# A two-layer trunk on one core: feed-forward activations and HGRN's heads turned by VectorE and DRAM in place of TensorE, and a new rule in the schedule

## The chip, the cores and the metric

The kernel runs on one core of one Trainium2 chip. The metric is device time in microseconds of one execution; the median of several executions is given. A profile is one execution recorded by the hardware profiler; its engines are PE (TensorE matmul), PEld (TensorE weight load), DVE (VectorE), ACT (ScalarE), POOL (GpSimd) and SP (SyncE, which issues DMAs).

## The reference

Input is x of 256 tokens by 2048 features, float32, batch 1. Two layers, each a token mixer and a SwiGLU feed-forward, each with RMSNorm before and a residual add behind, then one final RMSNorm:

```python
h = x
for layer in range(2):
    if layer == 0:
        h = h + gdn_mixer(rmsnorm(h, gdn_norm), ...)      # gated DeltaNet, 32 value heads of 128
    else:
        h = h + hgrn2_mixer(rmsnorm(h, hgrn_norm), ...)   # HGRN2, 16 heads of 128
    h = h + (silu(n @ w_gate) * (n @ w_up)) @ w_down      # n = rmsnorm(h, ffn_norm[layer]); inner width 5632
return rmsnorm(h, final_norm)
```

Both mixers project h, compute a chunked recurrence per head, normalize each head's output (`rmsnorm(o, head_norm) * silu(gate)`) and multiply it by an output matrix of their own.

## The kernel before, in words

All weights (some 500 MB) stream once from DRAM through SBUF. They come in *halves* of 128x1024 float32, loaded by SP's queue into four buffers `raw`. ScalarE copies a half to float32r (`wh`), VectorE subtracts (`wl = raw - wh`), four buffers each; TensorE multiplies high by high, high by low and low by high. `stream` loops over all groups of halves in the order of the computation and records load and split of a half three halves (`AHEAD`) before its matmuls. One half is 12 matmuls of 512 columns (row groups) or 24 of 256 (column groups, in which the weights stand still and the tokens move).

An activation that is multiplied next must stand with its features on partitions, split into a high and a low part as well: `xt_h`, `xt_l` for the normalized input, `ht` (`hth`, `htl` in the profile) for the feed-forward's inner activations, `ot_h`, `ot_l` for the mixers' heads. The turn from tokens on partitions to features on partitions is a TensorE transpose against the identity in tile `head`, block by block of 128x128, into a PSUM tile `aux`, from which ScalarE and VectorE write the two parts.

- `ffn`: 22 gate-up groups `gate_up(gi)` of four halves give 256 inner features each, in two parts (`FF_PARTS`, 12 and 10 groups); after each part four groups `down(part, cg)` of 12 or 10 halves multiply them, 512 output columns each. `gate_up`'s `end` runs ScalarE's Silu (`sg`) and VectorE's product (`h1`, the tile printed as `h`), and for every second group eight transposes `aux<-head,h` and the split of both groups' `ht`.
- `hgrn`: four head groups of projections f, q, v, gate; `hgrn_o` multiplies scores by values into `o`, and `head_out` normalizes the heads into `zs`, transposes them (eight `aux<-head,zs`) and splits them with the head norm as scale. Two output projections of four column groups follow.
- `gdn`: eight head groups in the order `GDN_ORDER`; `gdn_o` calls the same `head_out`.
- The residual lives in DRAM (`x_home`): `load_x` and `add_x` load and store 128x2x512 tiles through Pool's queue.

The order of instructions isn't that of the source. A `Recorder` takes down all operations; `plan` then simulates the five engines with fixed costs and gives out each engine's order. An operation gets a due time `late`, from the main stream of matmuls back through its successors; an engine takes of its ready operations the one due first. A DMA on Pool's queue counts 0.75 to issue and 6.5 to land (`ISSUE`, `LANDING`), and 0.2 (`HOP`) for a handover between engines. The engines then run in order, each in the planned sequence: an instruction that waits holds what is behind it. Nearly all instructions are issued in one place, so nearly all lines of the profile are L489 and the tile names tell them apart.

Of the kernel before, what the change touches and what calls it, by code (L numbers as in the profile page):

```python
# [17 lines left out]
P = 128  # L18
# [9 lines left out]
MASKED = (8, 4, 2, 1)  # L28
AHEAD = 3
RAW_BUFS = 4  # L30
SPLIT_BUFS = 4
# [47 lines left out]
class Op:  # L79
    __slots__ = ("eng", "method", "args", "kw", "cost", "lag", "main", "pred", "succ", "n", "late", "call", "tiles", "heirs", "share")  # L80

    def __init__(self, eng, method, args, kw, cost=0.0, lag=0.0, main=False):
        self.eng, self.method, self.args, self.kw = eng, method, args, kw
        self.cost, self.lag, self.main = cost, lag, main
        self.pred, self.succ = {}, []
        self.call, self.tiles, self.heirs = None, [], []
        self.share = 1.0


# [58 lines left out]
class Recorder:  # L148
    ENGINES = ("tensor", "vector", "scalar", "gpsimd", "sync")

    def __init__(self, scratch):
        self.scratch, self.tiles, self.ops, self.pools = scratch, {}, [], []
        self.last_main, self.wanted = None, []
        for e in self.ENGINES:
            setattr(self, e, Engine(self, e))
# [44 lines left out]
    def add(self, eng, method, args, kw):  # L200
        op = Op(eng, method, args, kw)
        op.n = len(self.ops)
        for other in self.wanted:
            self.edge(other, op)
# [102 lines left out]
    def plan(self):  # L307
# [22 lines left out]
        order = []  # L330
        table, streaming = None, False
        starved = {}
# [45 lines left out]
        while len(order) < len(ops):  # L378
# [127 lines left out]
class Trunk:  # L506
# [79 lines left out]
    def stream(self, groups):  # L586
# [10 lines left out]
        def load(n):  # L597
            g, i = flat[n]
            raw = self.tile(self.wraw, [P, 1024], "raw", ordered=True)
            nc.sync.dma_start(raw, g.halves[i])  # L600
            if n == 0:
# [5 lines left out]
            nc.vector.tensor_tensor(out=low, in0=raw, in1=h.bitcast(F32), op=ALU.subtract)  # L607
            ready[n] = (h, low)

        loaded = 0  # L610
        for n, (g, i) in enumerate(flat):
            while loaded < min(n + AHEAD, len(flat)):
                load(loaded)
                loaded += 1
            if i == 0:
                if g.begin:
                    g.begin()
                g.ps = self.apart() if g.apart else self.main()
            g.mm(g.ps, i, *ready.pop(n))
            if i == len(g.halves) - 1:  # L620
                g.end(g.ps)

    def mm_rows(self, ps, i, wh, wl, n_chunks, operand, halves=range(2)):

        for k in range(2):
            xh, xl = operand(2 * i + k)
            cols = slice(k * 512, (k + 1) * 512)
            for tt in halves:
                tok = slice(tt * P, (tt + 1) * P)
                out = ps[tt] if isinstance(ps, tuple) else ps[:, tt, :]  # L630
                for m, (s, w) in enumerate(((xh, wh), (xh, wl), (xl, wh))):
                    self.nc.tensor.matmul(
                        out, s[:, tok], w[:, cols],
                        start=(i == 0 and k == 0 and m == 0),
                        stop=(i == 2 * n_chunks - 1 and k == 1 and m == 2),
                    )
# [14 lines left out]
    def mm_cols(self, ps, i, wh, wl, n_k, n_f, n_chunks):  # L651

        for k in range(n_k):
            kt = i * n_k + k
            xh, xl = self.operand(kt)
            for f in range(n_f):
# [9 lines left out]
    def mm_gates(self, ps, i, wh, wl):  # L666
        for kt in range(16):
            xh, xl = self.operand(kt)
            at = slice(kt * 64, (kt + 1) * 64)
# [5 lines left out]
    def operand(self, kt):  # L675
        return self.xt_h[kt // 4][:, kt % 4, :], self.xt_l[kt // 4][:, kt % 4, :]

# [37 lines left out]
    def make_xt(self, cg, norm):  # L715
# [11 lines left out]
        for pair, ps in enumerate(two):  # L727
            for k in range(2):
# [4 lines left out]
                )  # L733

    def x_cols(self, x, cg):
        if x is self.a["x"]:
# [28 lines left out]
    def ffn(self, j, after):  # L765
        nc, a = self.nc, self.a
        hts, h1s = {}, {}

        def gate_up(gi):
            def end(ps):  # L770
                h1 = self.tile(self.pool, [P, 2, T], "h1", bufs=4)
                for tt in range(2):
# [13 lines left out]
                two = self.aux(), self.aux()  # L786
                nc.together(*two)
                for of, tr in enumerate(two):
                    for k in range(2):
                        for tt in range(2):  # L790
# [4 lines left out]
                for of, tr in enumerate(two):  # L795
                    ht, lt = (t[:, 2 * of : 2 * of + 2, :].rearrange("p a t -> p (a t)") for t in pair)
                    nc.scalar.activation(ht, tr, AF.Copy)
                    nc.vector.tensor_tensor(out=lt, in0=tr, in1=ht.bitcast(F32), op=ALU.subtract)

# [6 lines left out]
        def down(part, cg):  # L806
            first = sum(FF_PARTS[:part]) // 2
            n = FF_PARTS[part] // 2
            w = a[f"ffn_d{j}_{part}"]

            def operand(kt):
                h, l = hts[first + kt // 4]
                return h[:, kt % 4, :], l[:, kt % 4, :]

# [362 lines left out]

    def head_out(self, o, zs, scale, norm):

# [31 lines left out]
        for tt in range(2):  # L1211
            for h in range(4):
# [4 lines left out]
                )  # L1217
        oh, ol = (t([P, 4, T], f"ot_{x}", dt=F32R, bufs=3) for x in "hl")
        two = self.aux(), self.aux()
        nc.together(*two)  # L1220
        for b, tr in enumerate(two):
            for h in range(2):
                for tt in range(2):
                    nc.tensor.transpose(
                        tr[:, h * T + tt * P : h * T + (tt + 1) * P],
                        zs[:, tt, (2 * b + h) * P : (2 * b + h + 1) * P], self.ident,
                    )
        for b, tr in enumerate(two):
            s = slice(2 * b, 2 * b + 2)
            self.split_scaled(  # L1230
                oh[:, s, :].rearrange("p h t -> p (h t)"), ol[:, s, :].rearrange("p h t -> p (h t)"),
                tr, norm,
            )
# [88 lines left out]
    def out_proj(self, name, p, states, last, after):  # L1322
# [5 lines left out]
        def operand(kt):  # L1328
            h, l = two[kt // 4]["ot"]
            return h[:, kt % 4, :], l[:, kt % 4, :]  # L1330

# [214 lines left out]
    def hgrn_o(self, g, st):  # L1546
# [4 lines left out]
        for tok in range(2):  # L1551
            for h in range(4):
# [6 lines left out]
                )  # L1559
        st["ot"] = self.head_out(o, st["zs"], 0.5, self.hgrn_hn)  # L1560

# [192 lines left out]
```

## Time and profile before

| | |
|---|---|
| median of 3 executions | 2806.14 us (2805.82 to 2806.21) |
| the profiled execution | 2807.59 us, its span 2805.9 us |
| TensorE busy | 2786.4 us (99%) |
| VectorE, ScalarE, Pool busy | 1732.2, 1426.7, 251.3 us |
| granted clock of TensorE | 0.997 |
| DMA | 580.42 MB, mean 207 GB/s |

The span goes from the first to the last instruction; the execution's time has a little around it. Stages, read off the tile names: DeltaNet to about 820 us, feed-forward to about 1555, HGRN to about 2070, the second feed-forward to the end. A matmul's duration in the timeline covers its way through the array, so that neighbours overlap; the distance between starts is what one costs in a row. A group's "busy" is the union of its instructions' durations.

### The profile page before, as it was taken

To read this page: it belongs to the slowest core of one execution; us is meant where nothing else is said; L and a number is where in the kernel's file an instruction comes from. 1 tells how busy PE (TensorE), PEld (TensorE's weight loads), DVE (VectorE), ACT (ScalarE), POOL (GpSimd) and SP (SyncE) were. 2 spreads that over 40 slices of the span, in tenths; PEclk is the share of its full clock that TensorE was granted. 3 is DMA by queue.
4 is the path that set the end of the run, shared out by engine and by line. 5 is a ranking of instruction groups with operands and counts; after the bars stand their busy time and mean duration, and the time that the engine had idled before them with its cause. 6 is when DMAs were issued, how large, how long until landed. Compare 5 with 4: busy or idle time off the path is not lost.

```text
span 2805.9 us, 40816 instructions
## 1 busy us (share of the span) xinstructions
PE 2786.4 (99%) x15710; PEld 2374.5 (85%) x15710; DVE 1732.2 (62%) x2498; ACT 1426.7 (51%) x2016; POOL 251.3 (9%) x366
## 2 busy tenths in 40 slices
PE   9999999999999999999999999999999999999998
PEld 9988888887888888888888989989888888888887
DVE  6777888877755555445555677677555454454554
ACT  6646666564554444344444556556454444344443
POOL 1212222232110000000000100000100000000000
PEclk9999999999999999999999999999999999999999
DMA  7686678677776555665556645545775556665564
GB/s 254 199 274 210 211 226 261 215 220 241 239 221 211 192 189 188 225 222 190 188 189 218 215 163 170 173 160 165 246 258 191 191 188 207 222 208 189 189 199 158
DMA packets 162659, 580.42 MB, mean 207 GB/s; under 512 B 20138, under 2 KB 21306, under 8 KB 162336
## 3 DMA queue, kind: packets, MB, share of 16 engines
q1 hardware_dynamic: 138912, 503.15, 54.5%
q0 software_dynamic: 23264, 73.81, 8.4%
q8 instruction: 123, 2.02, 0.3%
q10 hardware_dynamic: 288, 0.85, 0.1%
q14 instruction: 72, 0.59, 0.1%
HBM read 550.42 MB, written 27.31 MB: 206 GB/s over the span
## 4 chain that ended last, share of the span: by engine, by line
PE 98%; DVE 1%; ACT 0%; issue 0%; DMA 0%; POOL 0%; SPq 0%; POOLq 0%; ACTq 0%
PE main L489 91%; PE aux L489 7%; ACT dec L489 0%; DMA first<-in_x 0%; DVE wl L489 0%; DVE utmp L489 0%; ACT wh L489 0%; DVE x L489 0%; DVE u L489 0%; DVE zs L489 0%; POOL ocol L489 0%; SPq L489 0%; DVE pre L489 0%; ACT xt_h L489 0%; DVE r L489 0%
## 5 line engine op out<-in xcount | busy, mean ns | idle before, releaser
L489 DVE TENSOR_TENSOR wl<-raw,wh 128x1024 fp32r<-128x1024 f32 x945 | 1158.2, 1226 | 982.8 <-ACT wh L489 980.6
L489 ACT ACTIVATE wh<-raw 128x1024 fp32r<-128x1024 f32 x945 | 1000.6, 1060 | 1260.8 <-PE main L489 1214.0
L489 PE MATMUL main<-wl,xt_h 128*128 128x512 f32 x2176 | 850.2, 391 | 2.7 <-DVE wl L489 2.7
L489 PE MATMUL main<-wh,xt_h 128*128 128x512 f32 x2176 | 852.0, 392 | 0.4 <-ACT wh L489 0.4
L489 PE MATMUL main<-wh,xt_l 128*128 128x512 f32 x2176 | 850.1, 391 | 0.0
L489 PEld LDWEIGHTS main<-wl,xt_h 128*128 128x128 f32 x2176 | 409.0, 188 | 86.5 <-DVE wl L489 3.5
L489 PEld LDWEIGHTS main<-wh,xt_h 128*128 128x128 f32 x2176 | 409.1, 188 | 83.9 <-ACT wh L489 0.8
L489 PEld LDWEIGHTS main<-wh,xt_l 128*128 128x128 f32 x2176 | 408.9, 188 | 83.8
L489 PE MATMUL main<-xt_h,wl 128*128 128x256 f32 (+1 forms) x1040 | 292.9, 282 | 0.9 <-DVE wl L489 0.9
L489 PE MATMUL main<-xt_l,wh 128*128 128x256 f32 (+1 forms) x1040 | 292.4, 281 | 0.3 <-DVE xt_l L489 0.3
L489 PE MATMUL main<-xt_h,wh 128*128 128x256 f32 (+1 forms) x1040 | 290.5, 279 | 0.0
L489 PE MATMUL main<-wh,hth 128*128 128x512 f32 x664 | 259.0, 390 | 0.0
L489 PE MATMUL main<-wh,htl 128*128 128x512 f32 x664 | 258.9, 390 | 0.0
L489 PE MATMUL main<-wl,hth 128*128 128x512 f32 x664 | 258.6, 390 | 0.0
L489 PEld LDWEIGHTS main<-xt_h,wh 128*128 128x128 f32 (+1 forms) x1040 | 196.0, 188 | 0.5 <-ACT wh L489 0.2
L489 PEld LDWEIGHTS main<-xt_h,wl 128*128 128x128 f32 (+1 forms) x1040 | 194.1, 187 | 1.3 <-DVE wl L489 1.1
L489 PEld LDWEIGHTS main<-xt_l,wh 128*128 128x128 f32 (+1 forms) x1040 | 194.0, 187 | 0.9 <-DVE xt_l L489 0.5
L489 PE MATMUL main<-wh,ot_l 128*128 128x512 f32 x384 | 151.9, 396 | 0.5 <-DVE ot_l L489 0.5
L489 PE MATMUL main<-wh,ot_h 128*128 128x512 f32 x384 | 151.5, 395 | 0.3 <-ACT ot_h L489 0.3
L489 PE MATMUL main<-wl,ot_h 128*128 128x512 f32 x384 | 150.8, 393 | 0.0
L489 PEld LDWEIGHTS main<-wh,hth 128*128 128x128 f32 x664 | 124.7, 188 | 25.7
L489 PEld LDWEIGHTS main<-wl,hth 128*128 128x128 f32 x664 | 124.7, 188 | 25.6
(209 smaller groups left out, 2181.7 us busy)
## 6 DMA issues: line engine op xcount, KB each, us to landing
raw<-in_ffn_gu SPq DMA_DIRECT2D x352, 512.0 KB, 3.6
raw<-in_ffn_d SPq DMA_DIRECT2D x176, 512.0 KB, 3.8
raw<-in_hgrn_in SPq DMA_DIRECT2D x128, 512.0 KB, 3.7
raw<-in_gdn_kq SPq DMA_DIRECT2D x64, 512.0 KB, 5.0
raw<-in_gdn_v SPq DMA_DIRECT2D x64, 512.0 KB, 4.5
raw<-in_gdn_z SPq DMA_DIRECT2D x64, 512.0 KB, 5.0
raw<-in_gdn_out SPq DMA_DIRECT2D x64, 512.0 KB, 4.7
x_home<-x POOLq DMA_DIRECT2D x36, 512.0 KB, 4.9
```

Source lines behind the costliest of these rows:

```text
L489: getattr(getattr(tc.nc, op.eng), op.method)(*args, **kw)
```

## The change

Three things change.

1. A new function `turn` replaces TensorE's transposes for the feed-forward (per gate-up group, no longer per pair) and for HGRN's heads. VectorE transposes all 32x32 blocks of a 128x512 (feed-forward) or 128x1024 (HGRN) tile into `blocks`; Pool's queue stores `blocks` to a DRAM tile `rows`, and four more DMAs of that queue, one for each band of 32 partitions, load it back over the source tile. ScalarE and VectorE then write the two parts from SBUF, through a view in runs of 32. For HGRN the values tile `v` serves as `blocks`, and the low part is written in four instructions. DeltaNet keeps its transposes, grouped by token half in place of head pair.
2. The turned tiles are laid out by token half ([128, 2, n, 128]), and the views that hand them to the matmuls follow that.
3. In `plan`, each split of a weight half carries the number of its half. ScalarE and VectorE take a ready split first if its half is at most one (`SOON`) past the half whose matmul was placed last. And a DMA on SP's queue of less than a fifth of a half counts 0.1 in place of 0.45.

```diff
@@ plan
-            op = heapq.heappop(ready[e])[2] if ready[e] else mains.pop()
+            soon = [x for x in ready[e] if x[2].half is not None and x[2].half <= half + SOON]
+            if soon and e in ("scalar", "vector"):
+                soon = min(soon, key=lambda x: x[2].half)
+                ready[e].remove(soon)
+                heapq.heapify(ready[e])
+                op = soon[2]
+            else:
+                op = heapq.heappop(ready[e])[2] if ready[e] else mains.pop()
...
+            if op.main:
+                half = op.half
...
-            clock[e] = at + max(0.45, LOAD_EVERY * op.share) if e == "sync" else done
+            clock[e] = at + max(0.1 if op.share < 0.2 else 0.45, LOAD_EVERY * op.share) if e == "sync" else done
@@ new
+    def turn(self, x, blocks):
+        nc = self.nc
+        width = x.shape[1] // 4
+        nc.vector.transpose(
+            blocks.rearrange("p (c a j) -> p a c j", c=4, j=32), x.rearrange("p (a c i) -> p a c i", c=4, i=32)
+        )
+        rows = self.tile(self.dram, [4, P, width], f"rows{width}", bufs=3)
+        nc.gpsimd.dma_start(rows.rearrange("c p a -> p c a"), blocks.rearrange("p (c a) -> p c a", c=4))
+        for c in range(4):
+            nc.gpsimd.dma_start(
+                x[32 * c : 32 * c + 32].rearrange("i (q a) -> i q a", q=4),
+                rows[c].rearrange("(q i) a -> i q a", q=4),
+            )
+        return x.rearrange("p (q a j) -> p a q j", q=4, j=32)
@@ ffn, gate_up
-                h1s[gi] = h1
-                if gi % 2 == 0:
-                    return
-                pair = hts[gi // 2] = tuple(
-                    self.tile(self.pool, [P, 4, T], f"ht{x}", F32R, bufs=max(FF_PARTS) // 2) for x in "hl"
-                )
...
-                            nc.tensor.transpose(
-                                tr[:, k * T + tt * P : k * T + (tt + 1) * P],
-                                h1s[gi - 1 + of][:, tt, k * P : (k + 1) * P], self.ident,
-                            )
...
+                blocks = self.tile(self.pool, [P, 512], "blocks", bufs=2)
+                turned = self.turn(h1.rearrange("p t c -> p (t c)"), blocks)
+                hts[gi] = ht, lt = tuple(
+                    self.tile(self.pool, [P, 2, 2, P], f"ht{x}", F32R, bufs=max(FF_PARTS)) for x in "hl"
+                )
+                as_turned = lambda x: x.rearrange("p t n (q j) -> p (t n) q j", q=4)
+                nc.scalar.activation(as_turned(ht), turned, AF.Copy)
+                nc.vector.tensor_tensor(
+                    out=as_turned(lt), in0=turned, in1=as_turned(ht.bitcast(F32)), op=ALU.subtract
+                )
@@ head_out, for HGRN
+        turned = self.turn(zs.rearrange("p t c -> p (t c)"), blocks)
+        as_turned = lambda x: x.rearrange("p t n (q j) -> p (t n) q j", q=4)
+        nc.scalar.activation(as_turned(oh), turned, AF.Copy, scale=norm)
+        for q in range(4):
+            nc.vector.scalar_tensor_tensor(
+                out=as_turned(ol)[:, :, q], in0=turned[:, :, q], scalar=norm,
+                in1=as_turned(oh.bitcast(F32))[:, :, q], op0=ALU.mult, op1=ALU.subtract,
+            )
```

More of the change, by code (lines that the diff above doesn't have):

```diff
@@ L29 @@
 AHEAD = 3
+SOON = 1
 RAW_BUFS = 4
@@ L79 @@
 class Op:
-    __slots__ = ("eng", "method", "args", "kw", "cost", "lag", "main", "pred", "succ", "n", "late", "call", "tiles", "heirs", "share")
+    __slots__ = ("eng", "method", "args", "kw", "cost", "lag", "main", "pred", "succ", "n", "late", "call", "tiles", "heirs", "share", "half")
     def __init__(self, eng, method, args, kw, cost=0.0, lag=0.0, main=False):
@@ L87, in __init__ @@
         self.share = 1.0
+        self.half = None
 class Virtual:
@@ L202, in add @@
         op.n = len(self.ops)
+        op.half = self.half
         for other in self.wanted:
@@ L330, in plan @@
         order = []
-        table, streaming = None, False
+        table, streaming, half = None, False, 0
         starved = {}
@@ L600, in load @@
             nc.sync.dma_start(raw, g.halves[i])
+            nc.half = n
             if n == 0:
@@ L607, in load @@
             nc.vector.tensor_tensor(out=low, in0=raw, in1=h.bitcast(F32), op=ALU.subtract)
+            nc.half = None
             ready[n] = (h, low)
@@ L618, in stream @@
                 g.ps = self.apart() if g.apart else self.main()
+            nc.half = n
             g.mm(g.ps, i, *ready.pop(n))
+            nc.half = None
             if i == len(g.halves) - 1:
@@ L632, in mm_rows @@
                     self.nc.tensor.matmul(
-                        out, s[:, tok], w[:, cols],
+                        out, s[:, tt, :], w[:, cols],
                         start=(i == 0 and k == 0 and m == 0),
@@ L654, in mm_cols @@
             kt = i * n_k + k
-            xh, xl = self.operand(kt)
+            xh, xl = (x.rearrange("p t j -> p (t j)") for x in self.operand(kt))
             for f in range(n_f):
@@ L667, in mm_gates @@
         for kt in range(16):
-            xh, xl = self.operand(kt)
+            xh, xl = (x.rearrange("p t j -> p (t j)") for x in self.operand(kt))
             at = slice(kt * 64, (kt + 1) * 64)
@@ L675, in operand @@
     def operand(self, kt):
-        return self.xt_h[kt // 4][:, kt % 4, :], self.xt_l[kt // 4][:, kt % 4, :]
+        return tuple(x[kt // 4][:, kt % 4, :].rearrange("p (t j) -> p t j", t=2) for x in (self.xt_h, self.xt_l))
     def sumsq(self, cg):
@@ L806, in down @@
         def down(part, cg):
-            first = sum(FF_PARTS[:part]) // 2
+            first = sum(FF_PARTS[:part])
             n = FF_PARTS[part] // 2
@@ L1217, in head_out @@
                 )
[L1218 to L1223, printed above, removed]
+        oh, ol = (t([P, 2, 4, P], f"ot_{x}", dt=F32R, bufs=3) for x in "hl")
+        if blocks is None:
+            two = self.aux(), self.aux()
+            nc.together(*two)
+            for tt, tr in enumerate(two):
+                for h in range(4):
                     nc.tensor.transpose(
-                        tr[:, h * T + tt * P : h * T + (tt + 1) * P],
-                        zs[:, tt, (2 * b + h) * P : (2 * b + h + 1) * P], self.ident,
-                    )
[L1228 to L1232, printed above, removed]
+                        tr[:, h * P : (h + 1) * P], zs[:, tt, h * P : (h + 1) * P], self.ident
+                    )
+            for tt, tr in enumerate(two):
+                s = lambda x: x[:, tt].rearrange("p n j -> p (n j)")
+                self.split_scaled(s(oh), s(ol), tr, norm)
+            return oh, ol
+        turned = self.turn(zs.rearrange("p t c -> p (t c)"), blocks)
[5 more added lines that the diff above has]
+                in1=as_turned(oh.bitcast(F32))[:, :, q], op0=ALU.mult, op1=ALU.subtract,
             )
```

25 lines of the change are left out of this document (8 added, 17 removed).

## The prediction

> **What bounds the kernel now.** I read the page first, its busy times and its chain that ended last:
>
> ```profile
> span 2805.9 us, 40816 instructions
> ...
> PE 2786.4 (99%) x15710; PEld 2374.5 (85%) x15710; DVE 1732.2 (62%) x2498; ACT 1426.7 (51%) x2016; POOL 251.3 (9%) x366
> ...
> PE 98%; DVE 1%; ACT 0%; issue 0%; DMA 0%; POOL 0%; SPq 0%; POOLq 0%; ACTq 0%
> ```
>
> TensorE is the chain: 98% of the span. So an instruction taken off TensorE shortens the kernel, unless what replaces it comes late. Next, the waits, those of ScalarE's weight split and of TensorE's weight loads for the main stream (columns: total us, times, longest):
>
> ```profile
> ACT wh L489 <- PE main L489: 1214.0, 810, 4.8
> ...
> PEld main L489 <- DVE wl L489: 4.6, 3, 2.6
> ...
> PEld main L489 <- ACT wh L489: 1.1, 2, 0.8
> ```
>
> ScalarE's splits wait for TensorE to free a buffer 810 times; TensorE waits for a split in five places. The split is done ahead, and the engines that do it have room. How much, by stage (columns: stretch, PE, PEld, DVE, ACT, POOL busy, clock, DMA share, GB/s; DeltaNet, then feed-forward):
>
> ```profile
> 140.00:700.00 560.00, 555.88 (x3552) 472.48 (x3551) 444.08 (x972) 336.65 (x601) 147.38 (x214) 1.00 0.73 232
> 850.00:900.00 50.00, 50.00 (x226) 41.53 (x225) 24.84 (x24) 21.67 (x25) 0.00 (x0) 1.00 0.60 200
> ```
>
> In the feed-forward, VectorE and ScalarE are half idle and Pool wholly, and TensorE has no gap and its full clock (1.00). In DeltaNet VectorE is at 79%.
>
> **Term 1: 176 feed-forward transposes leave TensorE.** They run in 22 batches of eight. One batch in the timeline of TensorE (start, duration):
>
> ```profile
> 890.31 0.39 PE L489 MATMUL main<-wh,xt_l 128*128 128x512 f32 x1
> 890.54 1.03 PE L489 MATMUL aux<-head,h 128*128 128x128 f32 x8
> 891.33 0.48 PE L489 MATMUL main<-wh,xt_h 128*128 128x512 f32 x1
> 891.65 0.40 PE L489 MATMUL main<-wl,xt_h 128*128 128x512 f32 x1
> 891.88 0.39 PE L489 MATMUL main<-wh,xt_l 128*128 128x512 f32 x1
> ...
> 914.78 0.39 PE L489 MATMUL main<-wl,xt_h 128*128 128x512 f32 x1
> ```
>
> And the groups of transposes (busy, mean ns, idle before):
>
> ```profile
> L489 PE MATMUL aux<-head,h 128*128 128x128 f32 x176 | 22.8, 272 | 0.0
> ...
> L489 PE MATMUL aux<-head,zs 128*128 128x128 f32 x96 | 12.9, 275 | 1.3 <-DVE zs L489 1.3
> ```
>
> Durations overlap, so I count starts. From 891.88 to 914.78 lie 101 undisturbed matmuls: 0.2267 us each. From 890.31 to 891.88 there are three, 0.68 us of the 1.57. The batch costs 0.89 us: 22 × 0.89 = **19.6 us**. The groups' 22.8 us would be too much, since it counts the overlap with the neighbours.
>
> **Term 2: HGRN's 32 transposes.** The second group's 96 are 12 batches; four are HGRN's and go, DeltaNet's eight stay (they are regrouped by token half, same count and shapes, nothing). One of the four:
>
> ```profile
> 1785.35 0.28 PE L489 MATMUL main<-xt_l,wh 128*128 128x256 f32 x1
> 1785.47 1.04 PE L489 MATMUL aux<-head,zs 128*128 128x128 f32 x8
> 1786.26 0.36 PE L489 MATMUL main<-xt_h,wl 128*128 128x256 f32 x1
> 1786.46 0.28 PE L489 MATMUL main<-xt_h,wh 128*128 128x256 f32 x1
> 1786.58 0.28 PE L489 MATMUL main<-xt_l,wh 128*128 128x256 f32 x1
> ```
>
> 1.23 us for three matmuls of 0.12: 0.87 us, four times **3.5 us**.
>
> **What replaces them.** No row shows this turn whole, so its steps are priced by the nearest rows, of the groups and, below, of the DMA issues (KB each, median us from issue to landing):
>
> ```profile
> L489 DVE TENSOR_TENSOR wl<-raw,wh 128x1024 fp32r<-128x1024 f32 x945 | 1158.2, 1226 | 982.8 <-ACT wh L489 980.6
> L489 ACT ACTIVATE wh<-raw 128x1024 fp32r<-128x1024 f32 x945 | 1000.6, 1060 | 1260.8 <-PE main L489 1214.0 <-PE aux L489 8.3 <-DVE utmp L489 8.1
> ...
> L489 DVE TENSOR_TENSOR htl<-aux,hth 128x512 fp32r<-128x512 f32 x44 | 28.2, 683 | 0.0
> ...
> L489 ACT ACTIVATE hth<-aux 128x512 fp32r<-128x512 f32 x44 | 23.5, 587 | 0.0
> ...
> L489 POOL DMA_DIRECT2D u<-u_dram x32 | 18.7, 590 | 13.0 <-issue 6.2 <-DMA u_dram<-u 6.2 <-POOL pre L489 0.5
> ...
> L489 DVE STREAM_TRANSPOSE inv<-u 32x256 f32<-32x256 f32 x32 | 13.8, 433 | 1.9 <-ACT u L489 1.0
> ...
> L489 POOL DMA_DIRECT2D u_dram<-u x8 | 7.4, 919 | 18.2 <-issue 12.2 <-DVE so L489 5.0 <-DVE u L489 1.0
> ```
>
> ```profile
> v_rows<-r POOLq DMA_DIRECT2D x8, 512.0 KB, 6.9
> ...
> u_dram<-u POOLq DMA_DIRECT2D x8, 128.0 KB, 4.4
> u<-u_dram POOLq DMA_DIRECT2D x32, 32.0 KB, 5.7
> ```
>
> VectorE's transpose of 128x512: the VectorE rows rise by 1.06 ns per element (683 at 512, 1226 at 1024), so 433 + 256 × 1.06 = 0.70 us. Per gate-up group (48 matmuls, 10.9 us) it is the one instruction that VectorE gains; the split of `ht` stays, one VectorE and one ScalarE instruction, from SBUF in runs of 32 (I take the 0.68 and 0.59 of before). By the feed-forward window VectorE goes from 24.84 to about 28 us of 50: covered, while the three halves of splits done ahead last. If it took three times as long, 2.1 us per group, VectorE would be at 34 of 50, still covered. In HGRN a transpose of 1024 (1.25 us) and four scaled subtractions replace two, four times in all: covered likewise.
>
> DMAs: per turn one store, and four loads which wait on it at the head of Pool's queue. DeltaNet sends its `u` the same way, so its rows are the nearest: store 4.4 to 6.9 us to landing, then three further issues of 0.59 and 5.7 for the last load. Round trip **11.9 to 14.4 us**; the schedule, with 0.75 per issue, 6.5 to land and 0.2 per handover, reckons 17.2. Pool's issues for 44 turns, (0.92 + 4 × 0.59) = 3.3 us each, fall where Pool shows no work; behind the waiting loads stand at most the loads and stores of the residual (`x`, `x_home`), which feed one addition per 10.9 us or slower. Traffic: each turn writes and reads its tile once, 0.5 MB per feed-forward group of 10.9 us, 48 GB/s beside the 200 of the window, on DMA engines 60% busy; DeltaNet's stage runs at 232 and 73%. Covered, by the weight loads' four buffers; at the worst a load that lands late shows as a wait of `wh` for a DMA.
>
> Who needs the result? Weight half i of a down group reads gate-up group i's turned tile. The tightest place is the last of part 1, before the tenth half:
>
> ```profile
> 2685.73 0.39 PE L489 MATMUL main<-wh,hth 128*128 128x512 f32 x1
> ...
> 2688.17 0.87 DVE L489 SCALAR_TENSOR_TENSOR h<-main,rstd,sg 128x256 f32<-128x256 f32 x2
> ```
>
> Down begins at 2685.73; nine halves of 12 × 0.2267 later, +24.5 us, that tile is read. `h` is done at +3.3. A weight split in front (1.23), the transpose (0.70), the longest round trip (14.4), a split in front on ScalarE (1.06) with its own 0.59, and the same on VectorE (1.23 + 0.68) give +23.2: hidden by 1.3 us at worst, and by some 7 with the shortest round trip and nothing in front. At the schedule's own 17.2 it would be 1.5 us late in two places: 3 us. Part 0, with twelve halves, has 5.4 us more. HGRN's last head group is needed by the second output projection, behind the first one's 16 weight halves (43.5 us): nothing.
>
> On this the Trainium skill, VectorE: DVE Perf Modes, § Rules for kernel authors, speaks against the change: for a 128×128 transpose it says to use TensorE if a PSUM destination is OK, which it was. By that rule these transposes would stay where they are and the sum would hold the ordering term alone, about 2802 us. The trace disagrees for this kernel: the batch's 0.89 us lie on the engine that is 99% busy.
>
> **Term 3: the order.** Putting ScalarE's and VectorE's weight split for the half in progress or the next first acts where a split was late. That is DeltaNet, ScalarE's timeline:
>
> ```profile
> 624.41 5.86 ACT L489 ACTIVATE dec<-g_row,shift 128x64 f32<-128x64 f32 x24 [0.16 <-PE aux L489]
> ...
> 632.98 3.88 ACT L489 ACTIVATE wh<-raw 128x1024 fp32r<-128x1024 f32 x4
> ```
>
> After 24 decay instructions, and the exponential behind them, four splits run in a row; TensorE stands meanwhile. All such places cost the 4.6 + 1.1 us of the weight loads' waits above: the gain is at most 5.7. From the other side, a split put in front delays the head group's own chain by 1.23 us; if each of eight head groups passed that on to TensorE, 9.8 us lost. I take −4, near the upper gain, since the rows show the very pattern that the rule breaks up. SP's shorter time for small DMAs concerns the 96 KB head load only: nothing. The operand views regroup the same 128 columns: nothing.
>
> **Sum.** 2805.9 − 19.6 − 3.5 − 4.0 = 2778.8 us of span. The profiled execution took 2807.59, 1.7 more than its span, and lies 1.45 above the median 2806.14. Against the median: **2779 us**, −1.0%.
>
> **Rivals.**
> (a) DeltaNet's order gets worse rather than better. For it: VectorE at 444 of 560 us there, and an order that changes everywhere. Against: the late splits are real. Term 3 becomes 0 to +9.8: 2783 to 2793.
> (b) The same, but so much that it eats the gain (27 us more waiting there, five times the 5.7 us that TensorE waits for splits now): about 2806. Nothing in the rows points to it but the crowded VectorE.
> (c) Slower: the turned data land after the place that the schedule gave to their split, and ScalarE and VectorE, which run in order, stand with the next weight splits behind them. The lead is three halves, 8.2 us, less a split on each engine (2.3): 5.9. It decides when the round trip passes 17.2 + 5.9 = 23.1 us; at 25 us each of 44 groups would lose 1.9, +84 us, so 2863; a loss over 0.2% needs 23.8. Against: the rows give 12 to 14.4. For: DeltaNet's Pool rows above hold "issue" idle of 12.2 us before the stores, time that no wait explains.
> Beside (c) stands the Trainium skill, SBUF — State Buffer, § SBUF: two separate sides: a DMA issued by GpSimd can't write its descriptors while VectorE runs an instruction that holds the shared port pair, "~620 ns alone", "~3100 ns" beside such a copy. Estimated by that page, five issues would add 12.4 us and the round trip would be 24 to 27. The trace gives no sign of it for VectorE's kinds of work here: Pool's loads of `u` take 590 ns on the mean.
>
> **Chances.** Forecast 0.68 (its own range 2775 to 2784, term 3 from −5.7 to 0 and 3 us at part ends), (a) 0.20, (b) 0.05, (c) 0.07. The range 2774 to 2792 reaches over the forecast and most of (a) and leaves out (b), (c) and the rim. What a measurement of this kernel can tell from no change is about 0.2%, 5.6 us. Faster 0.88, same 0.05, slower 0.07.
>
> **What would show it.** `aux<-head,h` gone, `aux<-head,zs` at 64, TensorE's rows at 0.2267 without a break through a feed-forward part; VectorE's new transposes near 0.70 us; round trips of 12 to 14 us and splits of `ht` that start without idle time before them; TensorE's waits for `wl` and `wh` in DeltaNet near nothing. I am wrong if TensorE waits for `htl` at part ends, if `wh` waits for a DMA, or if DeltaNet's stage ends later than now.

## The result, and the profile after

The changed kernel takes 2776.66 us (median of 4 executions, 2776.44 to 2776.76) against 2806.18 for the kernel before (2805.82 to 2806.24): a ratio of 0.9895 with a 95% interval of 0.9883 to 0.9906, 29.5 us less. The forecast was 2779, in a range of 2774 to 2792. The profiled execution took 2776.64 us.

The page of the changed kernel, its span, busy times and the chain that ended last (nearly all lines of the profile are now L501):

```profile
span 2774.9 us, 40981 instructions
...
PE 2759.1 (99%) x15502; PEld 2349.0 (85%) x15502; DVE 1766.1 (64%) x2554; ACT 1427.9 (51%) x2012; POOL 390.7 (14%) x606
...
PE 98%; DVE 1%; ACT 0%; DMA 0%; issue 0%; SPq 0%; POOLq 0%; POOL 0%; DVEq 0%; ACTq 0%
```

TensorE has 208 instructions fewer (176 + 32, the transposes), and the span is shorter by 31.0 us. TensorE is the chain as before. VectorE has 33.9 us more work, Pool 139.4, and ScalarE 1.2; none of it is in the chain.

The waits of the changed kernel (total us, times, longest):

```profile
ACT wh L501 <- PE main L501: 1197.4, 817, 3.9
...
PEld main L501 <- DVE wl L501: 2.1, 2, 1.2
...
ACT wh L501 <- DMA raw<-in_hgrn_out: 1.9, 1, 1.9
...
PEld main L501 <- ACT ot_h L501: 1.1, 1, 1.1
PEld main L501 <- DVE ot_l L501: 1.1, 1, 1.1
...
PEld main L501 <- DVE htl L501: 0.5, 2, 0.3
```

The weight splits still wait for TensorE, 817 times: they are still done ahead. Waits of the weight loads for `wl` fell from 4.6 to 2.1 us, those for `wh` are gone, and a new one for `htl`, the low part of a turned tile, is 0.5 us in two places. One split waits 1.9 us for a DMA, that of HGRN's output weights.

The groups of what replaces the transposes (busy, mean ns, idle before and its releaser):

```profile
L501 POOL DMA_DIRECT2D h<-rows x176 | 96.2, 554 | 204.5 <-issue 128.5 <-DMA rows<-blocks 70.8 <-ACT wh L501 5.3
...
L501 POOL DMA_DIRECT2D rows<-blocks x44 | 33.6, 763 | 642.6 <-DVE blocks L501 609.5 <-DVE wl L501 17.9 <-issue 15.2
L501 DVE STREAM_TRANSPOSE blocks<-h 128x512 f32<-128x512 f32 x44 | 31.0, 705 | 0.1
L501 DVE TENSOR_TENSOR htl<-h,hth 128x512 fp32r<-128x512 f32 x44 | 30.0, 682 | 0.0
...
L501 ACT ACTIVATE hth<-h 128x512 fp32r<-128x512 f32 x44 | 27.5, 625 | 0.0
...
L501 PE MATMUL aux<-head,zs 128*128 128x128 f32 x64 | 8.7, 274 | 0.0
...
L501 DVE STREAM_TRANSPOSE v<-zs 128x1024 f32<-128x1024 f32 x4 | 5.0, 1244 | 0.1
```

And their DMAs beside the weight loads (KB, median us from issue to landing):

```profile
raw<-in_ffn_gu SPq DMA_DIRECT2D x352, 512.0 KB, 4.7
raw<-in_ffn_d SPq DMA_DIRECT2D x176, 512.0 KB, 4.7
...
rows<-blocks POOLq DMA_DIRECT2D x44, 256.0 KB, 4.9
h<-rows POOLq DMA_DIRECT2D x176, 64.0 KB, 4.7
```

`hth` and `htl`, the two parts of a turned tile, start with no idle time before them (0.0 in the last column): whenever ScalarE and VectorE come to them, the data are there.

For "where did the time go" I compared, for the 12912 matmuls of the main stream, which stand in the same order in all kernels here, when the n-th one starts in each. For good, the lead over the kernel before grows only in these places (elsewhere in the two mixers it swings by up to some 3 us and comes back, where small matmuls stand at other places of the main stream):

| | DeltaNet | first feed-forward | HGRN | second feed-forward |
|---|---|---|---|---|
| lead gained, us | 7.7 | 9.69 | 3.48 | 9.68 |
| how | 1.47 near 300 us, 3.77 from 594 to 657, 2.42 from 759 to 819 | 11 steps of 0.892, less 0.12 | 4 steps of 0.87 | 11 steps of 0.892, less 0.13 |

With 0.1 us of an earlier start that is 30.65 of the span's 31.0 us.

### The profile page after: what moved, and what is told of

Its sections match the earlier page's. It is cut to its first block, busy times and chain, and to the rows that moved or that the text cites. A ratio compares the mean times of both kernels' runs of the same rounds, so it can differ in the third digit from the quotient of the medians.

```text
span 2774.9 us, 40981 instructions
## 1 busy us (share of the span) xinstructions
PE 2759.1 (99%) x15502; PEld 2349.0 (85%) x15502; DVE 1766.1 (64%) x2554; ACT 1427.9 (51%) x2012; POOL 390.7 (14%) x606
## 4 chain that ended last, share of the span: by engine, by line
PE 98%; DVE 1%; ACT 0%; DMA 0%; issue 0%; SPq 0%; POOLq 0%; POOL 0%; DVEq 0%; ACTq 0%
PE main L501 92%; PE aux L501 6%; DMA raw<-in_gdn_kq 0%; DVE wl L501 0%; ACT dec L501 0%; ACT wh L501 0%; SPq L501 0%; DVE zs L501 0%; DVE utmp L501 0%; DVE u L501 0%; DVE x L501 0%; ACT y L501 0%; POOLq L1779 0%; ACT junk L501 0%; DVE ot_l L501 0%
## 5 line engine op out<-in xcount | busy, mean ns | idle before, releaser
L501 DVE TENSOR_TENSOR wl<-raw,wh 128x1024 fp32r<-128x1024 f32 x945 | 1157.7, 1226 | 924.4 <-ACT wh L501 917.1
L501 ACT ACTIVATE wh<-raw 128x1024 fp32r<-128x1024 f32 x945 | 1000.9, 1060 | 1239.6 <-PE main L501 1197.4
L501 PE MATMUL main<-wl,xt_h 128*128 128x512 f32 x2176 | 848.8, 390 | 1.3 <-DVE wl L501 1.3
L501 PE MATMUL main<-wh,xt_l 128*128 128x512 f32 x2176 | 849.4, 390 | 0.0
L501 PE MATMUL main<-wh,xt_h 128*128 128x512 f32 x2176 | 848.6, 390 | 0.0
L501 PEld LDWEIGHTS main<-wl,xt_h 128*128 128x128 f32 x2176 | 408.5, 188 | 86.3 <-DVE wl L501 2.1
L501 PEld LDWEIGHTS main<-wh,xt_l 128*128 128x128 f32 x2176 | 408.5, 188 | 84.0
L501 PEld LDWEIGHTS main<-wh,xt_h 128*128 128x128 f32 x2176 | 408.6, 188 | 83.6
L501 PE MATMUL main<-xt_h,wl 128*128 128x256 f32 (+1 forms) x1040 | 292.3, 281 | 0.0
L501 PE MATMUL main<-xt_l,wh 128*128 128x256 f32 (+1 forms) x1040 | 291.8, 281 | 0.1
L501 PE MATMUL main<-xt_h,wh 128*128 128x256 f32 (+1 forms) x1040 | 289.9, 279 | 0.0
L501 PE MATMUL main<-wh,htl 128*128 128x512 f32 x664 | 258.8, 390 | 0.0
L501 PE MATMUL main<-wh,hth 128*128 128x512 f32 x664 | 258.3, 389 | 0.0
L501 PE MATMUL main<-wl,hth 128*128 128x512 f32 x664 | 258.3, 389 | 0.0
L501 PEld LDWEIGHTS main<-xt_h,wh 128*128 128x128 f32 (+1 forms) x1040 | 195.6, 188 | 0.3
L501 PEld LDWEIGHTS main<-xt_l,wh 128*128 128x128 f32 (+1 forms) x1040 | 193.8, 186 | 1.0 <-DVE xt_l L501 0.4
L501 PEld LDWEIGHTS main<-xt_h,wl 128*128 128x128 f32 (+1 forms) x1040 | 193.8, 186 | 0.2
L501 PE MATMUL main<-wh,ot_h 128*128 128x512 f32 x384 | 150.5, 392 | 0.8 <-ACT ot_h L501 0.8
L501 PE MATMUL main<-wh,ot_l 128*128 128x512 f32 x384 | 150.6, 392 | 0.6 <-DVE ot_l L501 0.6
L501 PE MATMUL main<-wl,ot_h 128*128 128x512 f32 x384 | 150.8, 393 | 0.0
L501 PEld LDWEIGHTS main<-wh,htl 128*128 128x128 f32 x664 | 124.6, 188 | 26.2 <-DVE htl L501 0.5
L501 PEld LDWEIGHTS main<-wh,hth 128*128 128x128 f32 x664 | 124.6, 188 | 25.9
```

The lines of the kernel that those rows point to most:

```text
L501: getattr(getattr(tc.nc, op.eng), op.method)(*args, **kw)
```

## Experiments

### The order and the turn apart

The first kernel is the one before with the new rule alone; the second is the changed one with the old rule. SP's count for small DMAs stays at 0.45 in both (the first expectation speaks of 0.1; the edit doesn't have it).

```diff
@@ plan (first: added to the kernel before; second: taken out of the changed one)
+            soon = [x for x in ready[e] if x[2].half is not None and x[2].half <= half + SOON]
+            if soon and e in ("scalar", "vector"):
+                soon = min(soon, key=lambda x: x[2].half)
...
```

> The kernel before, with the schedule's new rule alone (split of the half in progress or the next first on ScalarE and VectorE, and 0.1 us for small DMAs on SP's queue); no turn, no new layout. Theory: between the two traces the main stream gains 7.8 us inside DeltaNet and 23 us where the 26 batches of transposes are gone; the DeltaNet part is the rule's work at the places where ScalarE's decay block held back the weight splits. Then this kernel is 5 to 8 us faster than before (2798 to 2801 us), and its feed-forward and HGRN stages keep their length. Rival A: the 2.4 us at the end of DeltaNet come from the regrouped head transposes; then the rule alone gives 5.2 to 5.4 us (2801). Rival B: the rule gains nothing by itself and DeltaNet's gain comes from Pool's or VectorE's other work; then within 1.5 us of 2806.

> The changed kernel with the schedule's old rule (due time alone, 0.45 us for every DMA on SP's queue): the turn and the new layout stay. Theory: 26 batches of 0.89 us go, 0.1 to 0.3 us come back at the ends of part 1: 2806.2 - 23 = 2783 us, plus or minus 1.5 for DeltaNet's order, and TensorE waits for weight splits in DeltaNet as before (4 to 6 us of weight-load waits). Rival A: with the regrouped head transposes the end of DeltaNet is 2.4 us shorter as well: 2780.5. Rival B: the turn needs the new rule, since without it the turned splits displace weight splits in the feed-forward: over 2785, with waits of the main stream for wl or wh after DeltaNet.

The rule alone: 2799.98 us against 2806.16, ratio 0.9979 (0.9971 to 0.9988), 6.2 us less. The turn alone: 2782.81, ratio 0.9918 (0.9904 to 0.9931), 23.35 less. The two add up to the whole 29.5. By stages the rule gains 7.76 us in DeltaNet, in the same three places (1.47, 3.78, 2.42), and nothing behind it; its weight stream started 1.4 us later in that execution, a start that varies by about 1 us between executions. The turn gains 9.69, 3.47 and 9.69 in the first feed-forward, HGRN and the second feed-forward, as in the whole. In its trace it also has 2.7 in DeltaNet, though TensorE waits there as before; that is the clock, as is shown next.

The page of the kernel with the rule alone:

```profile
span 2799.7 us, 40818 instructions
...
PE 2783.3 (99%) x15710; PEld 2372.7 (85%) x15710; DVE 1732.8 (62%) x2498; ACT 1427.7 (51%) x2016; POOL 247.7 (9%) x366
```

The same 15710 instructions keep TensorE busy for 3.1 us less, and the span is 6.2 shorter: half of what the rule saves stood as busy time and in no wait. It is the granted clock. In the kernel before it falls to 0.5 for 3.41 us behind each of two stalls of DeltaNet (columns: stretch, PE, PEld, DVE, ACT, POOL busy, clock, DMA share, GB/s):

```profile
637.90:641.30 3.40, 3.40 (x11) 2.50 (x10) 2.84 (x12) 0.37 (x3) 0.00 (x0) 0.50 0.90 296
798.30:801.70 3.40, 2.93 (x8) 2.19 (x8) 1.24 (x2) 0.00 (x0) 0.00 (x0) 0.51 0.76 278
```

There matmuls of 512 columns start 0.42 us apart (at 799.53 and 799.95) in place of 0.227. With 3.40 and 2.93 us of busy time at half the clock, 1.7 and 1.5 us are lost, an estimate that meets the 3.1. The kernel with the rule alone and the changed one have no such stretch at these places. Neither has the kernel with the turn alone, in the execution that was traced, although it stalls like the kernel before (its wait for `wl`, and the stretch around the longest stall):

```profile
PE main L494 <- DVE wl L494: 3.7, 3, 2.3
```

```profile
633.00:645.00 12.00, 9.34 (x41) 6.93 (x40) 11.85 (x32) 7.12 (x14) 3.08 (x5) 1.00 0.72 253
```

It gains 1.64 and 1.26 us at the two places: those are its 2.7, less 0.2 at the start. So whether the clock falls behind such a stall differs between executions, and no run here shows what decides it. The kernel before has both kinds: its executions with a mean clock of 0.999 took 2804.5 to 2804.7 us, those with 0.997 took 2806.7 to 2807.8. Without these 2.7, rule and turn add in the traces too: 7.76 + 22.85, against 30.55 in the stages of the whole.

How the rule works shows in the changed kernel's ScalarE timeline, at the place that the prediction quoted (start, duration):

```profile
622.89 5.14 ACT L501 ACTIVATE dec<-g_row,shift 128x64 f32<-128x64 f32 x21 [0.16 <-PE aux L501]
627.93 1.04 ACT L501 ACTIVATE wh<-raw 128x1024 fp32r<-128x1024 f32 x1
628.88 0.81 ACT L501 ACTIVATE dec<-g_row,shift 128x64 f32<-128x64 f32 x3
...
632.39 2.94 ACT L501 ACTIVATE wh<-raw 128x1024 fp32r<-128x1024 f32 x3
```

One split now stands inside the block of 24 decay instructions. At DeltaNet's end it works in another way. VectorE's timeline before:

```profile
789.32 1.22 DVE L489 TENSOR_TENSOR x<-x,main 128x1024 f32<-128x1024 f32 x1 [3.10 <-PE main L489]
790.46 0.36 DVE L489 TENSOR_TENSOR so<-so,oscale 128x8 f32<-128x8 f32 x2
```

and with the rule alone:

```profile
783.19 0.37 DVE L501 TENSOR_TENSOR so<-so,oscale 128x8 f32<-128x8 f32 x2 [3.61 <-ACT junk L501]
...
787.64 2.15 DVE L501 SCALAR_TENSOR_TENSOR zs<-aux,ocol,zs 128x128 f32<-128x128 f32 x8
789.71 1.21 DVE L501 TENSOR_TENSOR x<-x,main 128x1024 f32<-128x1024 f32 x1
```

Before, the norm of the last heads (`so`) stood behind the residual's addition (`x`), which waited 3.10 us for TensorE. With the rule the norm and `zs` come first. The rule doesn't name these instructions; placing the splits otherwise put them in another order. TensorE's waits at this place fell only from 2.1 to 1.4 us, though (for `zs`, `ot_h`, `ot_l`); most of the 2.42 us gained here is the clock.

### The regrouped head transposes alone

The kernel before with the operand views and DeltaNet's transposes by token half, nothing else.

```diff
@@ head_out
-            for h in range(2):
-                for tt in range(2):
+            for tt, tr in enumerate(two):
+                for h in range(4):
                     nc.tensor.transpose(...)
```

> The kernel before with the new grouping of the head transposes alone (by token half in place of head pair, in DeltaNet and HGRN, and the layout that goes with it); feed-forward, HGRN's way of transposing and the schedule's rule as before. Theory: the grouping changes only which split TensorE meets first at the end of DeltaNet; 0 to 2.4 us faster (2803.8 to 2806.2), nothing elsewhere. Rival: the schedule comes out differently all over DeltaNet from this small edit, by more than 3 us to either side; then none of DeltaNet's 7.8 us can be put down to a rule.

2805.86 us (11 runs), ratio 1.0 (0.9991 to 1.0008). The lead moves by −1.25 from 594 to 657 us and by +1.31 at DeltaNet's end: nothing on the whole. Both are the clock again: in this execution it stands at 0.50 for 6.83 us from 635.6 on, and at 1.00 from 798 to 802. So the regrouping gains nothing, and the rule has its 2.42 us at DeltaNet's end without it; against this kernel, whose clock didn't fall there, 1.1 of them are left.

### How late may the data land?

Nothing in the DMAs changes here, only the time that the schedule reckons for them to land, 6.5 us in the changed kernel for store and load: with 2.0, 0.0 and 9.0 it puts `hth` and `htl` earlier, or later, in ScalarE's and VectorE's order.

```diff
-LANDING_OF = {"wide": 7.0, "u": 7.0}
+LANDING_OF = {"wide": 7.0, "u": 7.0, "rows128": 2.0, "rows256": 2.0, "h1": 2.0, "zs": 2.0}
```

> The changed kernel, with one number of the schedule's reckoning changed: a DMA of the turn counts 2.0 us to land in place of 6.5 (the stores to rows and the loads back). No work changes, only the order. The schedule then places the split of a turned tile some 8 us behind the transpose; the trace of the changed kernel shows the data there after 12.1 us in the middle, so ScalarE and VectorE, in order, stand some 4 us with the next weight splits behind them. Theory (the prediction's rival c): the lead of 5.9 us in the weight splits covers that: 2776.7 us within 1.5, and the short waits of TensorE for htl at the two ends of part 1 (0.13 us each) are gone. Rival: a wait on ScalarE reaches TensorE at once: 44 times 4 us, 2950.

> As the one before, with 0 us to land: the split of a turned tile is placed 4.2 us behind the transpose, its data come 8 us later than that. Theory: lead 5.9 us, so each of 44 groups loses 2 us: about 2865 us, with the main stream waiting for wh and wl in both feed-forwards. Rival A: the lead is more than my reckoning (three whole halves, 8.2 us, or four): no loss, 2777. Rival B: the wait passes on in full, over 3000.

> As the two before, but 9.0 us to land: the split is placed 22 us behind the transpose although the data are there after 12. Theory: the wait of TensorE at the ends of part 1 comes from the schedule's reckoning, not from the DMAs: the split would come some 5 us later than now, TensorE waits 4 to 5 us for htl at two places (part 0 has 5.4 us more and keeps clear): 2785 to 2787 us. Rival: the order of ScalarE and VectorE near the part's end is bound by the data's landing, and nothing changes: 2776.7.

| reckoned landing | median, us | ratio to before (interval) | against the changed kernel's 2776.66 |
|---|---|---|---|
| 2.0 | 2778.23 | 0.9898 (0.9885 to 0.9912) | +1.6 |
| 0.0 | 2810.95 (2806.57 to 2818.86) | 1.0021 (1.0011 to 1.003) | +34 |
| 9.0 | 2783.41 | 0.9917 (0.9904 to 0.9931) | +6.7 |

Waits with 2.0:

```profile
ACT hth L501 <- DMA h<-rows: 197.5, 43, 7.3
```

with 0.0:

```profile
ACT hth L501 <- DMA h<-rows: 325.5, 44, 8.3
...
PEld main L501 <- DVE wl L501: 35.1, 42, 1.6
...
PE main L501 <- DVE wl L501: 20.1, 34, 1.4
```

and with 9.0:

```profile
PE main L501 <- ACT hth L501: 3.3, 2, 1.7
...
PEld main L501 <- DVE htl L501: 2.1, 2, 1.0
```

With 2.0 ScalarE stands for the data in 43 of 44 groups, 4.7 us each in the median, and TensorE loses no more than one place of 1.7 us: the splits done ahead cover it. With 0.0 it stands 7.4 us per group, and the main stream loses 32.6 us, 3.2 of them in HGRN. Group by group the loss begins at a wait of about 6.8 us, and is what the wait has above that (7.02: 0.21; 7.47: 0.66; 8.01: 1.23): the lead is 6.8 us. At the start of the second feed-forward it is less: the one place that landing 2.0 lost is a wait of 7.34 there, which cost 1.72. That is rival (c)'s mechanism: the in-order engine that waits for a DMA holds the weight splits behind it. With 9.0 the schedule believes in a round trip of 22.2 us (17.2 + 2 × 2.5), and the last tile of part 1 is split too late for its reader: 4.3 us lost in the first feed-forward, 2.7 in the second. TensorE's two waits are the same in both, 1.67 and 0.61 us; the first place has 3.41 us at a clock of 0.50 behind them (from 1470.87 on), and loses 1.6 more. Reckoning too long costs as well as too short; from 2.0 to 6.5 the medians differ by no more than 1.6 us.

### DeltaNet's heads turned as well

Eight batches of transposes, one per head group, are left in DeltaNet, 0.87 us each by HGRN's price. The last group's result is needed at once, so seven are tried, with the value tile `r` (two buffers) as `blocks`, or, in a second kernel, with the single buffer of the decay's `g_row`.

```diff
-        st["ot"] = self.head_out(o, st["zs"], scale, self.gdn_hn)
+        st["ot"] = self.head_out(
+            o, st["zs"], scale, self.gdn_hn, r.rearrange("p t h d -> p (t h d)") if hg < 7 else None
+        )
```

> The changed kernel with DeltaNet's heads turned in the same way too, for head groups 0 to 6 (the eighth, whose result is wanted at once, keeps its TensorE transposes); the values tile r, dead by then, serves as blocks. Theory: seven more batches of 0.89 us leave TensorE and VectorE gets 7 times 1.7 us (transpose 1.25, four scaled subtractions 1.92 in place of two at 0.75) in a stage where it is at 79%: 2776.7 - 6.2 = 2770.5 us. Rival: Pool's queue in DeltaNet is in use (147 us busy of 560, and its loads wait there for their stores), so that the waiting loads of the turn hold back taps, before and u, and VectorE's chain comes late: gain under 3 us or a loss, with TensorE waiting for aux or wl in DeltaNet.

> The changed kernel with DeltaNet's heads turned as well, for head groups 0 to 6, as in the earlier run with r as blocks, but with blocks in the buffer of g_row. Theory: that earlier run lost 5.2 us at 205 to 267 us because r, kept until its store had landed, held back the next value group's evacuation from PSUM (the main stream waited for ACT r); with r free again the seven batches of 0.89 us show: 2770 to 2773 us, and no wait of main for r. Rival: VectorE's added 1.7 us per head group, or Pool's waiting loads, are what cost: then about 2779 again, with waits for wl or aux.

Through `r`: 2778.95 us, ratio 0.9904 (0.989 to 0.9917), 2.3 more than the changed kernel where 6.2 less was expected. Through `g_row`: 2866.52, ratio 1.0213 (1.0199 to 1.0227), 90 more; that expectation was missed widely.

With `r`, single gains show in mid-stage, but 5.15 us are lost between 205 and 267 us, 4.95 of them at one place, the start of the fifth key group. The timelines there, of Pool:

```profile
258.09 0.78 POOL L501 DMA_DIRECT2D rows<-r  x1 [0.67 <-DVE r L501]
261.96 0.30 POOL L501 MEMSET inv<- 32x256 f32 x1 [3.09 <-PE aux L501]
262.61 2.19 POOL L501 DMA_DIRECT2D zs<-rows  x4 [0.35 <-DMA rows<-r]
```

of ScalarE:

```profile
264.73 1.26 ACT L501 ACTIVATE r<-main,rstd 128x512 f32<-128x512 f32 x2
```

the same instructions of ScalarE in the changed kernel:

```profile
243.44 1.24 ACT L501 ACTIVATE r<-main,rstd 128x512 f32<-128x512 f32 x2
```

and of TensorE in the kernel with `r`:

```profile
262.81 1.08 PE L501 MATMUL aux<-u,pp 64*64 64x64 f32 x16 [0.94 <-ACT pp L501]
264.36 1.34 PE L501 MATMUL aux<-r,u 128*128 128x128 f32 x8 [0.47 <-ACT u L501]
266.05 0.39 PE L501 MATMUL main<-xt_h,wh 128*128 128x256 f32 x1 [0.35 <-ACT r L501]
```

One of the two `r` buffers is held as `blocks` until its store has landed, before 262.6. Only behind that, 21 us later than in the changed kernel, does ScalarE empty the third value group's product out of PSUM (`r<-main`), and TensorE's next key group, at 266.05, waits for it. Meanwhile TensorE does recurrence work (`aux`) out of its turn, in which it waits for 1.76 us; the rest of that work is taken from later places, and part of the loss comes back there (2.3 and 1.8 us by 323). VectorE is no busier there (45.5 of the 62 us from 205 to 267, against 47.8 in the changed kernel); a buffer lives longer.

With `g_row` the same thing is worse, as TensorE's waits show:

```profile
PE main L501 <- ACT zs L501: 23.2, 1, 23.2
...
PE aux L501 <- DVE inv L501: 19.7, 4, 16.3
```

The first group's turn comes at 354 us there, after `g_row` is free at last, and no matmul of the main stream starts between 289.6 and 370.9: 81 us are lost from 260 to 374 us. The longest wait, 23.2 us, belongs to the second place, where 39 us are lost from 607 to 702. It ends at 675.9, when a gate product that waited in PSUM gets one of the `zs` buffers that the turn holds. In both places the granted clock is 0.50 for much of the time (47.8, 23.9, 6.8 and 27.3 us), so a part of the loss is the clock's.

Which groups pay? The next three, with `r` again: the first group alone; groups 1 to 6; groups 1 to 6 with a shorter reckoned landing (4.8).

```diff
-            ... if hg < 7 else None
+            ... if hg == 0 else None        # first
+            ... if 0 < hg < 7 else None     # second, and third with "rows128": 4.8, "h1": 4.8 in LANDING_OF
```

> The changed kernel with DeltaNet's head group 0 turned, and no other. Theory: the loss of the earlier run sits in this one group's buffer r: 2776.7 + 5 - 0.9 = about 2780 us, with TensorE held at about 260 us by ACT r. Rival: one turn more is worth 0.9 us: 2775.8.

> The changed kernel with DeltaNet's heads turned as well for head groups 1 to 6 alone, r as blocks. Theory: of the seven groups of the earlier run only group 0 collides, since its r (two buffers) is wanted by the third value group, whose matmuls end while group 0's turn is on its way; from group 1 on the next use of the buffer is 40 us or more away. Without it six batches of 0.89 us show in full or nearly: 2771 to 2774 us, and no wait of the main stream for ACT r. Rival: VectorE's added work in DeltaNet costs what the batches give: 2776 to 2779.

> Head groups 1 to 6 turned as in gdn_r1to6, and a DMA of the turn in the feed-forward reckoned at 4.8 us to land (rows128 and h1) in place of 6.5. Theory: the split is then placed 13.8 us behind the transpose, a little behind the data's 12.1, and the two waits for htl at the ends of part 1 (0.13 us each) go: the same time as gdn_r1to6 within 1 us. Rival: at 13.8 us a part of the landings is later than the split, and weight splits behind it come late: 2 us or more above gdn_r1to6.

The first alone: 2778.46 us, ratio 0.9899 (0.9885 to 0.9914): it loses 5.8 between 205 and 267 us, in the place expected (the clock is 0.50 for 3.41 us from 263.9 on), and part comes back later. Groups 1 to 6: 2778.92, ratio 0.9903 (0.9888 to 0.9918), where 2771 to 2774 was expected: a miss. They gain 0.88, 0.89 and 0.69 in mid-stage, and lose 1.8 from 323 to 375, 2.6 near 690 and 3.5 from 702 to the stage's end, where TensorE's waits have one that wasn't there:

```profile
PE aux L501 <- DVE zs L501: 3.7, 1, 3.7
```

The 1.8 are the first group's collision again, which the theory had excluded: behind the store of the first turn `r<-main` starts at 364.5 us, 24 us later than in the changed kernel, and TensorE waits 2.6 us for it. At the two later places the clock falls to 0.50 for 3.41 us each, and the traced execution, 2782.0 us, is the slowest of the four: it loses 5.3 us on the changed kernel, the median 2.3.

With the shorter landing: 2780.13, ratio 0.9907 (0.9891 to 0.9924), no better. The waits for `htl` at part ends are gone from TensorE's list, but they were worth only 0.13 us each.

Last, the three groups in whose stretches nothing had been lost.

```diff
+            ... if 1 < hg < 5 else None
```

> The changed kernel with DeltaNet's head groups 2, 3 and 4 turned as well, r as blocks. Theory: in the run with groups 1 to 6 the batches' gain showed in the middle of DeltaNet, and the losses sat at group 1's place (1.8 us at 320 to 375 us) and from 650 us on, where the last head groups' chains came late. Groups 2 to 4 alone keep away from both: three batches of 0.89 us, 2774 us. Rival: any turn in this stage, whose ScalarE and VectorE have no lead to spare, moves the chains behind it and pays the batch back: 2776 to 2779.

2774.15 us (4 runs, 2773.89 to 2774.8), ratio 0.9886 (0.987 to 0.9903), span 2772.3. It is the fastest kernel of this study, 2.5 us under the changed one by the medians, about three batches' 2.6. The intervals of the two ratios overlap, and the two were timed in different sessions; that it is faster rests on the medians (each over its own runs of the kernel before: −32.2 and −29.5) and on the lead in the trace, 2.6 us at the end of DeltaNet, 0.3 of it from before the first turn.

## Why the prediction was right, and where its steps were off

**Term 1, the feed-forward's transposes: right.** −19.6 was said, 19.37 came: 22 steps of 0.892 us, less 0.25 at part ends. TensorE's rows run unbroken through where a batch stood (the first and the last of 38 rows in a row, 0.2268 us from start to start; from 860 to 1090 us no two starts are more than 0.227 apart):

```profile
887.72 0.39 PE L501 MATMUL main<-wl,xt_h 128*128 128x512 f32 x1
...
896.11 0.39 PE L501 MATMUL main<-wh,xt_l 128*128 128x512 f32 x1
```

The groups' busy time would have said 22.8: starts, not durations, gave the right price.

**Term 2, HGRN: right.** −3.5 said, 3.48 measured. `aux<-head,zs` stands at 64.

**Term 3, the order: the direction right, the size wrong.** −4 said, at most −5.7; the rule alone gains 6.2 by the medians and 7.76 on the main stream. The step that was too small is "All such places cost the 4.6 + 1.1 us": those are the weight loads' waits for `wl` and `wh`, of which 3.6 us went (2.1 are left for `wl`). It took a stall to cost its wait and no more. In the traced execution of the kernel before two stalls were followed by 3.41 us at half the clock each, about 3.2 us together, which no wait row shows and which are gone with the rule. It also left out the waits for the heads at DeltaNet's end, 0.7 us of the gain. The three make 7.5 of the 7.76. The clock's part depends on the execution, so that the medians show less, 6.2; that this lies so near the upper bound of 5.7 is luck, as that bound counts other things. It is also the term by which the forecast of 2779 us lies above the 2776.66. The bound from the other side, 9.8, and with it rival (a), didn't show: no stretch of DeltaNet lost lead for good. SP's new count left no trace: without it the rule has the same three gains.

**The turn's costs: hidden, as said.** VectorE's transposes take 705 and 1244 ns (0.70 and 1.25 said). The round trip, from the transpose's end to the landing of the last load, is 12.1 us in the median, 9.0 to 14.3 in the feed-forward (11.9 to 14.4 said), and up to 17.2 for one of HGRN's. ScalarE's part of the split takes 625 ns where I took 587, for nothing. The row of the loads, `h<-rows`, has 128.5 us of "issue" idle, the sign that the prediction held for rival (c). It is the wait for the store: the first load starts 0.28 to 0.57 us behind the landing of its store, in all turns but one (2.13).

One count was wrong, here and in the description of the kernel: a gate-up group has eight halves, four chunks of features with two halves each, 96 matmuls and 21.8 us, and not four halves and 10.9 us. Successive `blocks` transposes are 21.76 us apart. So VectorE's extra work and the DMA traffic per unit of time are half of what I reckoned (24 GB/s in place of 48). It was an error toward caution and changes no term.

**Part ends: nearly.** The last tile of part 1, in the second feed-forward, on VectorE:

```profile
2661.00 0.71 DVE L501 STREAM_TRANSPOSE blocks<-h 128x512 f32<-128x512 f32 x1
...
2680.04 0.68 DVE L501 TENSOR_TENSOR htl<-h,hth 128x512 fp32r<-128x512 f32 x1
```

on ScalarE, and its reader on TensorE:

```profile
2678.77 0.61 ACT L501 ACTIVATE hth<-h 128x512 fp32r<-128x512 f32 x1
```

```profile
2680.78 0.50 PE L501 MATMUL main<-wh,htl 128*128 128x512 f32 x1
```

The data had landed 11.8 us after the transpose; `hth` starts 17.06 after it, where the schedule's 17.2 put it, as in nearly all groups (17.77). So the real margin is set by the reckoned time and not by the DMA. I had priced that case at 1.5 us late in each of two places. It was 0.13: I had added a weight split in front of ScalarE's part on top of the reckoned round trip, and it had run within it; `htl` is also read only by the third matmul of its half, 0.45 us after the first.

**Rival (c): real, but not here.** With the lead it would have decided at 17.2 + 5.9 = 23.1 us; the measured lead is 6.8, and the longest round trip, 17.2, is at the limit of no wait at all. By the 5.9 a landing of 0.0 would have cost more than it did.

**Signs of being wrong.** Two of the prediction's three showed, both too small to matter: TensorE waits for `htl` at part ends (0.25 us of lead), and `wh` waits for a DMA, 1.9 us in HGRN, where the lead shows no step.

**The rules of the Trainium skill.** VectorE: DVE Perf Modes, § Rules for kernel authors, would keep 128×128 transposes on TensorE if a PSUM destination is OK. A kernel by that rule was run, the order alone: 2799.98 us, 23.3 slower than with the turn. On a TensorE that is 99% busy the measurement decides against it. SBUF — State Buffer, § SBUF: two separate sides, would have a DMA that Pool issues take "~3100 ns" beside a VectorE copy that holds the shared port pair. Here, with VectorE 64% busy, the turn's issues take 554 and 763 ns on the mean and 812 at most: no sign of it.

## What to carry to other kernels

Where one in-order engine is 98% of the chain, a batch on it is worth what it adds from start to start, and moving it off pays even by a path ten times as long (12.1 us for 0.89), if the reader comes later than that path. An instruction that waits for a DMA on an engine that also feeds the bound may wait as long as that engine's prefetch leads, here 6.8 us, so the time that a schedule reckons for the landing has to be neither far too short nor far too long. A stall of the bounding engine can cost more than its wait: behind some of them TensorE ran 3.41 us at half the clock, which shows as busy time only. And what stops such a trick is less the busy time of the other engines than the buffers that it holds longer: find which product waits for that buffer before extending it to the next stage.

## What was not expected of the hardware

- The weight loads of the feed-forward land 4.7 us after issue where it was 3.6 and 3.8, with 27 MB more traffic in all. No split of the feed-forward waits for them.
- VectorE's 32x32 transposes cost what an ordinary pass over float32 costs, by 1.05 ns per element of a row ((1244 − 705) / 512), beside 1.06 for the splits.
- The start of the weight stream differs by about 1 us between executions of kernels that are the same up to there; it is in every difference of two single traces. In the two traces where it starts latest, at 10.2 and 10.4 us (landing 2.0 and the rule alone), the granted clock is 0.5 for 3.41 us from 8.5 and 8.7 on.
- Inside the kernels the stretches at a clock of 0.5 last 3.41 us or a multiple of it (6.83, 23.89, 27.31, 47.79), and each stands where TensorE waits or has just waited. Not every such wait brings one: the same 2.3 us did in the kernel before, and did not with the turn alone.
